# Thirty-seven low parts built by an accumulating transfer, and one modulation vector moved from TensorE to VectorE

## The chip, the cores and the metric

The program runs on one core of a Trainium2 chip. The metric is the device time of one execution in microseconds (us), here the median of three runs. Five engines work side by side, each through its own queue in order: TensorE (PE, with its weight loads as PEld), VectorE (DVE), ScalarE (ACT), GpSimd (POOL) and SyncE (SP), which here only issues transfers. Sixteen DMA engines move the data.

## The reference, cut to what is computed

Two groups of 128 tokens (context and latent) pass through two layers with the same weights. A layer is a half-step SwiGLU FFN, a token mixer of three branches (a Mamba-2 scan, differential attention, multi-scale pooling), and a second FFN. Each of the three sub-layers takes a normalised input that is shifted, scaled and gated by vectors made from the conditioning:

```
mod = silu(cond) @ w_ada[l] + b_ada[l]          # nine vectors of 1024
h = modulate(rmsnorm(x, g[0]), mod[0], mod[1])
x = x + 0.5 * mod[2] * swiglu(h, ffn_w_in[l, 0], ffn_w_out[l, 0])
h = modulate(rmsnorm(x, g[1]), mod[3], mod[4])
x = x + mod[5] * mixer(h)
h = modulate(rmsnorm(x, g[2]), mod[6], mod[7])
x = x + 0.5 * mod[8] * swiglu(h, ffn_w_in[l, 1], ffn_w_out[l, 1])
```

All weights are float32, and the whole of them is read once.

## The kernel before, in words

All weights of the products lie in HBM as 486 tiles of 128 x 1024 float32 (512 KB) in the order of their use (`plan`). The text numbers them 0 to 485. The order is, for each layer: 44 tiles `fin` (FFN input) and 22 `fout`, then the mixer's 111 tiles, then 44 `fin` and 22 `fout` again. The stretches that the change touches are the mixer of layer 0 from its keys on (tiles 113 to 168), the second FFN of layer 0 (177 to 242) and the first FFN of layer 1 (243 to 308).

A product is made with three matmuls in place of one. Each weight tile is split into a high part `wh` (a cast to float32r by ACT, `emit_hi`) and a low part `wl` (the raw tile minus the high part, by DVE, `emit_lo`), and the input into `xh` and `xl`; `mm3` adds wh·xh, wh·xl and wl·xh in PSUM. So a tile costs PE 24 matmuls, ACT one cast and DVE one subtraction.

SP loads the raw tiles into four buffers. High parts are made up to `HI_AHEAD` = 5 tiles and low parts up to `LO_AHEAD` = 4 tiles ahead of the tile that PE is to start next, both from `end`, which follows the issue of each tile's matmuls. `wh` and `wl` have five buffers each, so a cast for tile u waits until PE has done with tile u - 5. A raw buffer is free again when the subtraction has read it; the next load is asked for at that point (`load_more`).

The modulation vectors are made in two ways. `ada_stream` loads an eighth of one (512 KB, `wada`) and multiplies it on PE into the tile `pa` (four float32 matmuls, which the trace shows as eight rows). `ada_rows` loads an eighth of its transpose (`wrow`) and makes it on DVE: two `scalar_tensor_tensor` over 128 x 1024 with an accumulated sum, one for each group. The table `ROWS` lists the vectors (layer, number) made in this second way, and `CAP` how many of its eighths each stretch may take; whatever is left in the list goes to the next stretch.

Side work (modulation, norms, attention, the scan) is put between the tiles by `Pace`, a planner that keeps an estimated clock for each engine while the program is built. What it decides is fixed in the program: on the chip each queue runs in that order.

In a `fin` stretch the first pairs of tiles (`HYB` = 8 pairs, 16 tiles, in the stretches above) are multiplied before the row factors of the norm are known, and DVE puts these in when it reads PSUM (`wide`); beside them `full_h` makes the normalised input, eight pieces, each through POOL (`t1k<-x,rb`), DVE and ACT. The text calls these 16 tiles the hybrid stretch. The row factor itself passes through POOL (`rsr`, a power) just before it.

Of the kernel before, what the change touches and what calls it, by code (L numbers as in the profile page):

```python
# [12 lines left out]
AF = mybir.ActivationFunctionType  # L13
ALU = mybir.AluOpType
# [22 lines left out]
OFF_K = 3616  # L37
# [11 lines left out]
LO_AHEAD = 4  # L49
# [10 lines left out]
FIRST = 5.0  # L60
FH_ACT = False
FEED_ACT = 0
ROWS = ((0, 5), (0, 6), (0, 7), (0, 8), (1, 0), (1, 2), (1, 3), (1, 4), (1, 5), (1, 6), (1, 7), (1, 8))
CAP = {(0, 0): (5, 9), ("mix", 0): (18,), (0, 1): (16, 10), (1, 0): (16, 10), ("mix", 1): (18,), (1, 1): (12, 0)}
MIX_END = 2
MIX0 = 1
HOLD = 5
END = 6
ROW_LAG = 0.7
ROW_RAMP = 0.0  # L70
# [116 lines left out]
def ada_plan(seq):  # L187
# [5 lines left out]
    def spread(mods, u0, u1):  # L193
        items = [m + (k,) for m in mods if m not in ROWS for k in range(KD)]
        rest.extend((int(u0 + (u1 - u0) * j / len(items)), it) for j, it in enumerate(items))
# [13 lines left out]
def rows_plan(seq):  # L209
    def at(*head):  # L210
        return next(u for u, s in enumerate(seq) if s[:len(head)] == head)

    def even(n, a, b):
        return [a + j * (b - a) // n for j in range(n)]

    plan = {}
    for key, n in CAP.items():
        if key[0] == "mix":
            e = at("wout", key[1])
            us, last = even(n[0], at("win", key[1], OFF_K) + MIX0, e - MIX_END), e  # L220
        else:
            a = at("fin", *key)
            us = even(n[0], a + IN0, a + 2 * KF - 4) + even(n[1], a + 2 * KF, a + 3 * KF - END)
            last = a + 3 * KF
        plan[key] = us, last
    return plan


def pack_rows(w_ada):
    return np.stack([w_ada[l, :, i * D:(i + 1) * D].T.reshape(KD, P, D) for l, i in ROWS])  # L230

# [96 lines left out]
class Pace:  # L328

    LAT = {"pe": 0.25, "dve": 0.13, "act": 0.17, "pool": 0.2, "dma": 2.2}

    def __init__(self):
        self.clk = {"pe": 0.0, "dve": 0.0, "act": 0.0, "pool": 0.0, "dma": 0.0}
        self.wr = {}
        self.acc = {}
        self.last = {}
        self.born = {}
        self.slots = {}  # L340
# [22 lines left out]
    def op(self, eng, cost, outs, ins):  # L363
# [14 lines left out]
        for a in outs:  # L378
            r = self.wr.setdefault(a.tensor.name, {})
            lo, hi = self.span(a)  # L380
            for k in [k for k in r if lo <= k[0] and k[1] <= hi]:
                del r[k]
            r[lo, hi] = t + self.LAT[eng]

# [40 lines left out]
def backbone(ctx: ExitStack, tc: tile.TileContext, seq, wst, wada, wa0, wrow, xT_d, cT_d, cB_d, ck_d, cv_d, h0_d, prm_d, cst_d,  # L425
             y_d, nk_d, nv_d, ns_d):
    nc = tc.nc
    pace = Pace()
    clk = pace.clk
    V, S, T_, G = (Paced(pace, n, e) for n, e in  # L430
                   (("dve", nc.vector), ("act", nc.scalar), ("pe", nc.tensor), ("pool", nc.gpsimd)))
# [13 lines left out]
    def nm(s):  # L445
        uid[0] += 1
        return f"{s}{uid[0]}"
# [4 lines left out]
    def big(dt=F32):  # L452
        return bigx(dt)[:, 0:1024]
# [78 lines left out]
    def advance():  # L532
        again = True
        while again:
            again = False
            for lst, n in ((side["first"], 99), (side["gens"], CONC), (side["slow"], 99)):
                for s in list(lst[:n]):
                    if due(s) and step_side(s, lst):
                        again = True
                        break  # L540
                if again:
                    break
# [12 lines left out]
    def add(gen, first=False):  # L555
        side["first" if first else "gens"].append(Side(gen))

    def misc(gen):
        add(gen, True)

    raws = {}
    wt = {}
    st = {"load": 0, "cap": T0, "hi": 0, "lo": 0, "cur": 0}

    def load(out, src):
        nc.sync.dma_start(out=out, in_=src)
        pace.op("dma", out.free_size() * P * 4 / 360e3, [out], [])
# [5 lines left out]
    def load_more(limit):  # L573
        while st["load"] < min(limit, st["cap"]):
            i = st["load"]
            raws[i] = pace.slot("raw", RAW_BUFS, wp.tile([P, 1024], F32, tag="raw", bufs=RAW_BUFS, name=nm("raw")))
            load(raws[i], wst[i])
            st["load"] += 1

    def emit_hi():  # L580
        u = st["hi"]
        if u < T0:
            hi = big(F32R)
        else:
            hi = pace.slot("wh", WH_BUFS, wp.tile([P, 1024], F32R, tag="wh", bufs=WH_BUFS, name=nm("wh")))
        S.copy(hi, raws[u])
        wt[u] = [hi, None]
        st["hi"] += 1

    def emit_lo():  # L590
        u = st["lo"]
        if u < T0:
            lo = big(F32R)
        else:
            lo = pace.slot("wl", WL_BUFS, wp.tile([P, 1024], F32R, tag="wl", bufs=WL_BUFS, name=nm("wl")))
        V.tensor_tensor(out=lo, in0=raws.pop(u), in1=wt[u][0], op=ALU.subtract)
        wt[u][1] = lo
        st["lo"] += 1
        load_more(st["lo"] + RAW_BUFS)

    def use(desc):
        u = st["cur"]
        assert seq[u] == desc, (seq[u], desc)
        while st["hi"] <= u:
            emit_hi()
        while st["lo"] <= u:
            emit_lo()
        st["cur"] += 1
        hi, lo = wt.pop(u)
        return hi, lo  # L610

    def end(later=(), swap=False, less=0):
        cur = st["cur"]
        if not swap:
            for fn in later:
                fn()
            advance()
        while st["hi"] < min(cur + HI_AHEAD - less, len(seq)) and st["hi"] in raws:
            emit_hi()
        while st["lo"] < min(cur + LO_AHEAD - less, st["hi"]):  # L620
            emit_lo()
        if swap:
            for fn in later:
                fn()
        advance()
# [65 lines left out]
    row_plan = rows_plan(seq)  # L691
    row_todo = [m + (j,) for m in ROWS for j in range(KD)]

# [3 lines left out]
    def ada_rows(us, last):  # L697
# [10 lines left out]
        while True:  # L708
            if not row_todo or st["cur"] >= last - HOLD:
                us.clear()  # L710
            if us and len(loaded) < 2 and us[0] <= st["cur"] + 2:
                u, item = us.pop(0), row_todo.pop(0)
                raw = big()
                load(raw, wrow[ROWS.index(item[:2]), item[2]])
                loaded.append((u, item, raw))
# [164 lines left out]
    def ffn_in(l, f, box=None, pre=()):  # L880
# [47 lines left out]
        for p in range(KF):  # L928
            if p == HYB[l, f]:
                settle(lambda: "h" in box)  # L930
            if p % 2 == 0:
                cat.append(big(F32R))
            for which in range(2):
                ps = pre.pop(0) if pre else mtile(("fin", l, f, which * KF + p), hs if p >= HYB[l, f] else fh)
                pend.append((evac_u if which else evac_g, p, ps))
                later = []
                if box["rb"] is not None:
                    while pend:
                        fn, pi, t = pend.pop(0)
                        later += fn(pi, t)  # L940
                end(later, SWAP_I)
            if l == 0 and f == 0 and p == T_SIDE:
                side["slow"].append(Side(ada_rows(*row_plan[l, f]), row_lag))
                side["slow"].append(Side(ada_stream()))
            if l == 0 and f == 0 and p == T_SETUP:
                add(setup_consts())
                add(setup_layer(0))
        return out

    def ffn_out(l, f, acts, nxt):  # L950
# [3 lines left out]
        for m in range(KD):  # L954
            ps = pmain(2 * NT if m < KD - 1 else NT)
            for k in range(KF):
                if not cur:
                    if n:
                        end(later, SWAP_F, FO_LESS[max(0, n + 7 - KF)])
                        later = []  # L960
                    cur = tiles8(use(("fout", l, f, n)))
                    n += 1
                wh, wl = cur.pop(0)
                xh, xc = acts[k]
                if m == KD - 1:
                    T_.matmul(ps, lhsT=wh, rhs=xh, start=(k == 0), stop=False)
                    T_.matmul(ps, lhsT=wh, rhs=xc[:, NT:], start=False, stop=False)
                    T_.matmul(ps, lhsT=wl, rhs=xh, start=False, stop=(k == KF - 1))
                    if k % SUB == SUB - 1:
                        advance()  # L970
                    continue
                if k < KF - 1:
                    T_.matmul(ps, lhsT=wh, rhs=xc, start=(k == 0), stop=False)
                T_.matmul(ps[:, 0:NT], lhsT=wl, rhs=xh, start=False, stop=False)
                if k == KF - 1:
                    T_.matmul(ps, lhsT=wh, rhs=xc, start=False, stop=True)
                if k % SUB == SUB - 1:
                    advance()
            later += gated_add(l, 2 if f == 0 else 8, m, [ps[:, 0:NT], ps[:, NT:]] if m < KD - 1 else [ps], nxt, m == KD - 1)
        end(later)  # L980

    def setup_consts():
# [723 lines left out]
    def split():  # L1706
        emit_hi()
        emit_lo()
# [128 lines left out]
```

## Time and profile before

| | |
|---|---|
| median of three runs | 1553.76 us (1552.73 to 1557.59) |
| the profiled execution: its own time | 1555.05 us |
| its span, first to last instruction | 1553.2 us, TensorE's granted clock 0.998 of full |
| TensorE busy | 1513.9 us, 97% |
| VectorE busy | 1303.5 us, 84% |
| ScalarE busy | 864.5 us, 56% |
| GpSimd busy | 60.7 us, 4% |
| read from HBM | 342.00 MB, 223 GB/s over the span |

The span is what the trace covers, and 1.85 us of the execution's own time lie around it. Busy shares are means over the whole program; the stretches differ.

### The profile page before, as it was taken

What the parts mean: (1) busy time and instruction counts of PE and PEld (TensorE: products, weight loads), DVE (VectorE), ACT (ScalarE), POOL (GpSimd) and SP (SyncE); (2) the same over time, 40 slices, a digit from 0 to 9 for tenths busy, and PEclk for the clock granted to TensorE, in tenths of its full rate; (3) what the DMA queues carried; (4) which work ended last, traced back from release to release, by engine and by line L of the source; (5) the groups of instructions that cost most, each with busy time, mean ns of one, the idle gap of its engine ahead of it and who ended that gap; (6) DMA issues with size and microseconds to landing.
All of it is one profiled execution on the core that took longest, in us unless ns stands there. A gap on an engine that the chain in (4) does not pass through costs nothing. (4 is left out here: it accounts for less than half of the span.)

```text
span 1553.2 us, 30573 instructions
## 1 busy us (share of the span) xinstructions
PE 1513.9 (97%) x11934; PEld 1421.0 (91%) x11934; DVE 1303.5 (84%) x2404; ACT 864.5 (56%) x1560; POOL 60.7 (4%) x65
## 2 busy tenths in 40 slices
PE   6999999999999999999999999999999999999997
PEld 4998889989979999899899998998897999999986
DVE  5777798986888998899989999898778989998664
ACT  3564447665576446644446544577556744665442
POOL 0000002000001000100001000110000020010000
PEclk9999999999999999999999999999999999999999
DMA  9698775553765666688766887555467568568652
GB/s 373 224 338 287 264 265 166 188 187 131 246 214 190 220 240 221 209 297 286 265 215 200 288 279 269 189 179 186 158 213 229 189 204 287 172 201 279 211 181 82
DMA packets 103345, 350.30 MB, mean 226 GB/s; under 512 B 11424, under 2 KB 19232, under 8 KB 103072
## 3 DMA queue, kind: packets, MB, share of 16 engines
q1 hardware_dynamic: 103200, 348.34, 65.9%
q8 instruction: 94, 1.54, 0.4%
q14 instruction: 51, 0.42, 0.1%
HBM read 342.00 MB, written 4.19 MB: 223 GB/s over the span
## 5 line engine op out<-in xcount | busy, mean ns | idle before, releaser
L394 PE MATMUL pm<-big,wh 128*128 128x256 f32 (+2 forms) x6568 | 1289.6, 293 | 4.3 <-DVE big L394 2.5
L394 PEld LDWEIGHTS pm<-big,wh 128*128 128x128 f32 x6568 | 1028.0, 189 | 53.3 <-issue 20.2
L394 PE MATMUL pm<-big,wl 128*128 128x256 f32 (+1 forms) x3592 | 1003.6, 281 | 0.0
L394 PEld LDWEIGHTS pm<-big,wl 128*128 128x128 f32 x3592 | 676.6, 188 | 2.3
L394 DVE TENSOR_TENSOR wl<-raw,wh 128x1024 fp32r<-128x1024 f32 x481 | 587.8, 1227 | 14.8 <-ACT wh L394 14.4
L394 ACT CAST wh<-raw 128x1024 fp32r<-128x1024 f32 x481 | 502.5, 1050 | 137.4 <-PE pm L394 87.6
L394 DVE SCALAR_TENSOR_TENSOR big<-big,big 128x1024 f32<-128x1024 f32 x198 | 241.9, 1222 | 12.8 <-DMA big<-wrow 11.4
L394 ACT CAST big<-t1k 128x256 fp32r<-128x256 f32 x88 | 36.0, 409 | 156.3 <-DVE t1k L394 156.3
L394 PE MATMUL pm<-wh,big 128*128 128x512 f32 x256 | 86.2, 401 | 2.0 <-ACT big L394 2.0
L394 ACT ACTIVATE big<-x,amod 128x128 fp32r<-128x128 f32 x96 | 33.5, 397 | 96.7 <-DVE x L394 79.1
L394 DVE TENSOR_TENSOR wide<-pm,rb 128x258 f32<-128x258 f32 (+1 forms) x108 | 45.2, 422 | 36.8 <-PE pm L394 33.3
L394 DVE SCALAR_TENSOR_TENSOR x<-pm,mods,x 128x128 f32<-128x128 f32 x152 | 43.7, 345 | 36.4 <-PE pm L394 36.2
L394 PEld LDWEIGHTS pm<-wh,big 128*128 128x128 f32 x256 | 48.2, 188 | 15.0 <-ACT big L394 2.9
L394 ACT COPY big<-pm 128x256 f32<-128x256 f32 (+2 forms) x88 | 30.8, 374 | 50.3 <-PE pm L394 50.0
L394 DVE TENSOR_TENSOR big<-t1k,big 128x256 fp32r<-128x256 f32 x128 | 55.7, 440 | 1.6 <-ACT big L394 0.9
L394 ACT ACTIVATE t1k<-wide 128x128 f32<-128x128 f32 (+1 forms) x96 | 33.6, 397 | 38.9 <-DVE wide L394 38.6
L394 PE MATMUL pm<-wl,big 128*128 128x512 f32 x128 | 50.3, 393 | 0.0
L394 PE MATMUL s<-big,big 128*64 128x128 f32 (+5 forms) x416 | 46.3, 312 | 1.5 <-ACT big L394 1.5
L394 ACT ACTIVATE t1k<-pm 128x256 f32<-128x256 f32 x58 | 22.4, 386 | 43.8 <-PE pm L394 43.8
L394 POOL TENSOR_TENSOR rsr<-rsv,halfc 128x2 f32<-128x2 f32 x9 | 6.3, 698 | 919.0 <-DVE rsv L394 919.0
L394 DVE TENSOR_TENSOR t1k<-pm,t1k 128x256 f32<-128x256 f32 x42 | 17.8, 424 | 28.6 <-PE pm L394 26.7
L394 DVE SCALAR_TENSOR_TENSOR big<-big,cw,big 128x252 f32<-128x252 f32 (+1 forms) x96 | 39.4, 485 | 2.8 <-ACT big L394 2.8
(146 smaller groups left out, 977.7 us busy)
## 6 DMA issues: line engine op xcount, KB each, us to landing
raw<-wst SPq DMA_DIRECT2D x486, 512.0 KB, 4.2
big<-wrow SPq DMA_DIRECT2D x96, 512.0 KB, 5.6
big<-wada SPq DMA_DIRECT2D x32, 512.0 KB, 5.6
big<-wa SPq DMA_DIRECT2D x16, 512.0 KB, 10.2
big<-cB SPq DMA_DIRECT2D x12, 512.0 KB, 7.4
big<-big SPq DMA_DIRECT2D x32, 64.0 KB, 5.2
x<-xT SPq DMA_DIRECT2D x1, 1024.0 KB, 4.9
big<-h SPq DMA_DIRECT2D x2, 512.0 KB, 5.2
```

The source lines that it names most:

```text
L394: r = fn(*a, **k)
```

## The change

For 37 tiles (`DMA_LO`, `dma_plan`) DVE's subtraction is taken out. In its place ACT writes the negated high part into the `wl` buffer, and POOL issues a transfer that reads the raw tile from HBM a second time and adds it to what stands there. The raw buffer of such a tile is given back when the cast has read it. These tiles' low parts are begun one tile earlier than the others. They are 13 tiles in the mixer of layer 0 (115, 119, ... 163), 14 in the second FFN of layer 0 (181, 185, ... 233) and 10 in the first FFN of layer 1 (247, 253, ... 301). The vector (1, 1), eight eighths, joins `ROWS` and so goes from PE to DVE; `CAP` is the same. The planner gets a clock for the new transfers.

```diff
-ROWS = ((0, 5), (0, 6), (0, 7), (0, 8), (1, 0), (1, 2), (1, 3), (1, 4), (1, 5), (1, 6), (1, 7), (1, 8))
+ROWS = ((0, 5), (0, 6), (0, 7), (0, 8), (1, 0), (1, 1), (1, 2), (1, 3), (1, 4), (1, 5), (1, 6), (1, 7), (1, 8))
...
+DMA_LO = (
+    (("win", 0, OFF_K, 2), ("wout", 0, -4), 4),
+    (("fin", 0, 1, 4), ("fin", 0, 1, 60), 4),
+    (("fin", 1, 0, 4), ("fin", 1, 0, 60), 6),
+)
...
+def dma_plan(seq):
+
+    def at(*head):
+        return next(u for u, s in enumerate(seq) if s[:len(head)] == head)
+
+    plan = set()
+    for a, b, step in DMA_LO:
+        plan.update(range(at(*a[:-1]) + a[-1], at(*b[:-1]) + b[-1], step))
+    return plan
...
-    LAT = {"pe": 0.25, "dve": 0.13, "act": 0.17, "pool": 0.2, "dma": 2.2}
+    LAT = {"pe": 0.25, "dve": 0.13, "act": 0.17, "pool": 0.2, "dma": 2.2, "acc": 4.0}
...
-        V.tensor_tensor(out=lo, in0=raws.pop(u), in1=wt[u][0], op=ALU.subtract)
+        if u in by_dma:
+            raws.pop(u)
+            S.activation(out=lo, in_=wt[u][0], func=AF.Copy, scale=-1.0)
+            nc.gpsimd.dma_start(out=lo, in_=wst[u], accum_op=ALU.add)
+            pace.op("acc", 1.5, [lo], [lo])
+        else:
+            V.tensor_tensor(out=lo, in0=raws.pop(u), in1=wt[u][0], op=ALU.subtract)
...
-        while st["lo"] < min(cur + LO_AHEAD - less, st["hi"]):
+        while st["lo"] < min(cur + LO_AHEAD + (st["lo"] in by_dma) - less, st["hi"]):
```

The order of the instructions shows three places. The first is PE in the input stretch of layer 0's second FFN, tile 211, where the eighth and last item of vector (1, 1) stands before (`pa`).

```order
L394 MATMUL pm_8819<-big_7449,wh_8667 128x256
L394 MATMUL pm_8819<-big_7447,wl_8704 128x256
L394 MATMUL pa_7414<-big_8753,silc 32x256 x4
L394 MATMUL pm_8819<-big_7447,wh_8667 128x256
L394 MATMUL pm_8819<-big_7449,wh_8667 128x256
L394 MATMUL pm_8819<-big_7447,wl_8704 128x256
```

After the change no row with `pa` stands in this stretch; the eight before are at tiles 176 to 211.

The second is ACT in the hybrid stretch of layer 1's first FFN, at tile 253. Before:

```order
L394 CAST wh_10060<-raw_9905 128x1024
L394 ACTIVATE big_9827<-t1k_10042,mods_83,amod_85 128x128 x2
L394 CAST big_10013<-t1k_10055 128x256
L394 CAST wh_10104<-raw_9956 128x1024
L394 ACTIVATE t1k_10136<-wide_10137 128x128 x2
L394 CAST wh_10141<-raw_10002 128x1024
```

And of the change:

```order
L410 CAST wh_10053<-raw_9898 128x1024
L410 ACTIVATE big_9824<-t1k_10029,mods_83,amod_85 128x128 x2
L410 CAST big_10006<-t1k_10048 128x256
L410 CAST wh_10097<-raw_9949 128x1024
L410 ACTIVATE wl_10103<-wh_10097 128x1024
L410 ACTIVATE t1k_10137<-wide_10138 128x128 x2
L410 CAST wh_10142<-raw_9995 128x1024
```

The negation stands right behind its cast, ahead of the SiLU of the next pair.

The third is POOL at the start of layer 0's second FFN: the row factor (`rsr`), the pieces of `full_h` (`t1k<-x,rb`) and, of the change, the transfers of tiles 181 and 185.

```order
L616 DMA wl_7499<-wst 128x1024
L410 TENSOR_TENSOR rsr_7509<-rsv_7507,halfc 128x2
L410 TENSOR_TENSOR t1k_7601<-x,rb_7564 128x256
L410 TENSOR_TENSOR t1k_7603<-x,rb_7564 128x256
L616 DMA wl_7646<-wst 128x1024
L410 TENSOR_TENSOR t1k_7653<-x,rb_7564 128x256
```

Before, POOL's queue has no transfer at all; now the row factor stands behind one, and the third to eighth piece of `full_h` behind another.

## Rows read from the trace of the kernel before

**Rows 1.** Page, parts 1 and 2: busy us (share) xinstructions; GB/s in 40 slices.
```profile
PE 1513.9 (97%) x11934; PEld 1421.0 (91%) x11934; DVE 1303.5 (84%) x2404; ACT 864.5 (56%) x1560; POOL 60.7 (4%) x65
PEclk9999999999999999999999999999999999999999
GB/s 373 224 338 287 264 265 166 188 187 131 246 214 190 220 240 221 209 297 286 265 215 200 288 279 269 189 179 186 158 213 229 189 204 287 172 201 279 211 181 82
```

**Rows 2.** Waits of PE: us in total, times, longest us.
```profile
PE pa L394 <- DMA big<-wada: 4.6, 5, 1.3
...
PE pm L394 <- DVE wide L394: 1.7, 6, 0.5
```

**Rows 3.** PE's instructions on tile pa, 596 to 725 us.
```profile
L394 PE MATMUL pa<-big,silc x64: 379/391/403, 603.5 to 715.9; 128*32 128x256 f32 x64
```

**Rows 4.** Timeline of PE at 715 us: start us, us, instruction.
```profile
715.47 0.28 PE L394 MATMUL pm<-big,wl 128*128 128x256 f32 x1
715.68 0.64 PE L394 MATMUL pa<-big,silc 128*32 128x256 f32 x8
716.25 0.50 PE L394 MATMUL pm<-big,wh 128*128 128x256 f32 x2
716.59 0.28 PE L394 MATMUL pm<-big,wl 128*128 128x256 f32 x1
```

**Rows 5.** Groups of instructions, shapes apart: busy us, mean ns | idle before.
```profile
L394 DVE TENSOR_TENSOR wl<-raw,wh 128x1024 fp32r<-128x1024 f32 x481 | 587.8, 1227 | 14.8 <-ACT wh L394 14.4
L394 DVE SCALAR_TENSOR_TENSOR big<-big,big 128x1024 f32<-128x1024 f32 x198 | 241.9, 1222 | 12.8 <-DMA big<-wrow 11.4 <-ACT big L394 0.4
...
L394 ACT ACTIVATE big<-big 128x1024 f32<-128x1024 f32 x18 | 18.7, 1058 | 0.4 <-DVE big L394 0.4
...
L394 DVE DVE_READ_ACCUMULATOR big<-big,big 128x1 f32 x192 | 16.2, 85 | 0.0
```

**Rows 6.** Windows: stretch, PE, PEld, DVE, ACT, POOL busy us, PEclk, DMA share, GB/s.
```profile
615.00:650.00 35.00, 33.14 (x272) 31.12 (x271) 32.00 (x66) 24.98 (x49) 5.97 (x8) 1.00 0.64 211
655.00:742.70 87.70, 85.46 (x735) 82.52 (x734) 77.30 (x122) 39.36 (x60) 0.00 (x0) 1.00 0.83 293
815.00:850.00 35.00, 34.78 (x291) 34.61 (x291) 33.84 (x69) 24.34 (x47) 4.78 (x7) 1.00 0.58 192
```

**Rows 7.** Transfers of the raw tiles: KB each, median us to landing; their range.
```profile
raw<-wst SPq DMA_DIRECT2D x486, 512.0 KB, 4.2
DMA to landing us min/median/max: 3.4/4.2/11.2
```

**Rows 8.** Timeline of ACT: the casts of tiles 189, 209 and 253.
```profile
638.88 1.05 ACT L394 CAST wh<-raw 128x1024 fp32r<-128x1024 f32 x1
...
696.37 1.05 ACT L394 CAST wh<-raw 128x1024 fp32r<-128x1024 f32 x1
...
829.45 1.06 ACT L394 CAST wh<-raw 128x1024 fp32r<-128x1024 f32 x1
```

**Rows 9.** Timeline of PE: first matmul with wl of tiles 189, 209 and 253.
```profile
645.88 0.29 PE L394 MATMUL pm<-big,wl 128*128 128x258 f32 x1
...
708.08 0.28 PE L394 MATMUL pm<-big,wl 128*128 128x256 f32 x1
...
834.63 0.28 PE L394 MATMUL pm<-big,wl 128*128 128x258 f32 x1
```

**Rows 10.** Timeline of POOL and DVE at 825 us, layer 1's hybrid stretch.
```profile
825.18 0.74 POOL L394 TENSOR_TENSOR t1k<-x,rb 128x256 f32<-128x256 f32 x1 [1.30 <-DVE t1k L394]
...
825.25 1.75 DVE L394 TENSOR_TENSOR wl<-raw,wh 128x1024 fp32r<-128x1024 f32 x1
...
829.02 1.22 DVE L394 TENSOR_TENSOR wl<-raw,wh 128x1024 fp32r<-128x1024 f32 x1
```

More of the change, by code (lines that the diff above doesn't have):

```diff
@@ L328 @@
 class Pace:
-    LAT = {"pe": 0.25, "dve": 0.13, "act": 0.17, "pool": 0.2, "dma": 2.2}
+    LAT = {"pe": 0.25, "dve": 0.13, "act": 0.17, "pool": 0.2, "dma": 2.2, "acc": 4.0}
     def __init__(self):
-        self.clk = {"pe": 0.0, "dve": 0.0, "act": 0.0, "pool": 0.0, "dma": 0.0}
+        self.clk = {"pe": 0.0, "dve": 0.0, "act": 0.0, "pool": 0.0, "dma": 0.0, "acc": 0.0}
         self.wr = {}
@@ L559, in misc @@
         add(gen, True)
+    by_dma = dma_plan(seq)
     raws = {}
```

## The prediction, made before the run

> **What bounds the kernel now.** I read the page's busy line and slices first. TensorE is busy 97% of the span, 1513.9 of 1553.2 us, at a clock of 9 tenths or more in every slice [rows 1]; VectorE has 84% and ScalarE 56%. So the end is set by TensorE's work plus the few microseconds in which it waits, and anything else counts only where it makes TensorE wait. The waits of PE come next. One entry is tied to what the change touches: the items of vector (1, 1) wait for their loads, 4.6 us in five waits, the longest 1.3; waits on VectorE's `wide` are 1.7 us in six [rows 2]. No wait for a `wl` or a `wh` is large enough to stand there. The windows show where a second engine is close: VectorE is busy 32.0 of 35 us and 33.84 of 35 in the two hybrid stretches, and 77.3 of 87.7 in the rest of layer 0's second FFN; ScalarE has at least 10 us free in each [rows 6].
>
> **What PE loses: 10.1 us.** The eight items are the 64 rows of `pa` from 603.5 to 715.9 us [rows 3]. Row busy times overlap on PE, so I take starts. From the matmul ahead of the last item (715.47) to the one behind it (716.25) pass 0.78 us [rows 4]; without it two neighbours start some 0.12 apart (1513.9 us of PE over 11934 matmuls are 0.127 each [rows 1]). So an item costs 0.66, eight 5.3. With them go the waits for their loads, 4.6 [rows 2], and two small transposes of the finished vector, some 0.2 together. Sum 10.1. These loads become eight of the same size in the same queue, `wrow` for `wada`, so I price the bytes at nothing.
>
> **What VectorE, ScalarE and SP get: nothing, under cover.** VectorE loses 37 subtractions of 1.227 and gains 16 row products of 1.222 with a read of 0.085 behind each [rows 5]: -45.4 + 20.9 = -24.5 us. It is covered already outside the hybrid stretches, and no row product of the eight falls inside one. ScalarE gains 37 negations. The nearest row is its 128 x 1024 activation, 1.058 us [rows 5], so +39; the negation reads float32r in place of float32, and I see no reason for less. In the busiest place it goes from 24.98 to about 30 of 35 us. If that cover is gone, each negation makes the evacuation behind it 1.06 late. The raw buffer is given back by the cast, about 2 us earlier than by the subtraction, which can only help the next load.
>
> **POOL.** Its queue had no transfer among these pieces; now the row factor stands behind tile 181's and six pieces of `full_h` behind 185's. Each transfer must wait for its negation, and what stands behind it waits too. Both negations come well before the pieces are needed; I price it at 0, and at up to 2 us for the range.
>
> **The new wait: 4.1 us.** A low part was made 1.2 us after its cast; now it takes a negation and a transfer of which no row exists. Call L the time from the end of the negation to the landing. Bounds are the shortest and the longest landing of a raw tile of the same 512 KB, 3.4 and 11.2 [rows 7]. I start at their median, 4.2. To add, the transfer must also read what stands in `wl`: 0.52 MB at the highest rate of any slice, 373 GB/s [rows 1], is 1.4; a handover between the engines 0.2. L = 5.8, near the lower bound because the median is.
>
> What a tile can afford is the first matmul with its `wl` less the end of its cast less 1.06. For tile 209, a steady one: 708.08 - (696.37 + 1.05) - 1.06 = 9.6 [rows 8, 9]. In the same way from the casts and first matmuls of all 37, 33 lie between 8.2 (tile 229) and 13.0 (tile 143). Four, in the hybrid stretches, are short. Tile 253: 834.63 - 830.51 - 1.06 = 3.06. Tile 189: 645.88 - 639.93 - 1.06 = 4.89; two items ahead of it are gone, 1.7 plus waits of 0.5, so PE is there 2.2 us earlier, while its cast comes 1.7 earlier (one subtraction of 1.75, beside POOL, is gone): about 4.4. Tile 259 has 4.95, and gains 1.65 by 253's subtraction and by the wait at 253. Tile 185 has 6.66, less 0.8 for PE's earlier arrival. At L = 5.8 tile 253 waits 2.7 and tile 189 1.4; 185 and 259 just hold. That is 4.1.
>
> The same list gives the price at other L (a wait lengthens the budget of the next such tile by as much): 1.2 at 4.2, 5.0 at 6.1, 6.8 at 7, 8.8 at 8, then 17 at 9 (15 tiles late), 25 at 9.5 (22 late) and 52 at 11. It is nearly flat until the steady tiles begin to be late, between 8.2 and 9, and steep after.
>
> **The term on `wide`: -0.9.** Of PE's 1.7 us [rows 2] about half lies in the stretches that VectorE gets relief in; I take 0.9.
>
> **Sum.** -10.1 + 4.1 - 0.9 = -6.9. The profiled execution took 1555.05: 1553.2 of span and 1.85 around it, 1.29 above the median of the runs. So 1548.2 for a profiled execution of the same sort, and 1546.9 to the median: I say 1547.0.
>
> **A rule of the pages against it.** Beside a POOL piece that started at 825.18, a subtraction took 1.75 us; a later one alone 1.22 [rows 10]. So POOL and VectorE hinder each other here, by 0.5 us. The Trainium skill ("SBUF — State Buffer", "SBUF: two separate sides") says that GpSimd writes the descriptors of the transfers it issues through ports that it shares with VectorE, and that a VectorE operation in a two-port mode locks it out; its example goes from about 620 to about 3100 ns. The trace agrees that the two engines collide, and does not show a transfer held up. What it would do is the third rival below. The same notes ("DMA: Bandwidth & Descriptors", "Anatomy of one DMA — SWDGE (gpsimd) path") fit such a transfer as 2.0 us plus the bytes at 436 GB/s; an estimate from that page for 512 KB is 3.2, and by it tile 253 alone would wait, some 0.1, and the sum would be -10.9, 1543. My L is the higher one because raw tiles take 4.2 here [rows 7].
>
> **The rivals.** *Quick transfers:* L below 5. Then B is 1.2 to 2.5, time 1543 to 1545.5. For: 3.4 is the shortest landing. Against: the median, and the second operand. Chance 0.12.
>
> *What is freed is handed back:* the two items in layer 0's hybrid stretch (at about 622 and 642 us) make up some 2.9 of the 10.1. VectorE works 32 of 35 there [rows 6] and PE cannot outrun it; PE then waits on `wide` for those 2.9, and the time is 1550 to 1551. Against: three or four subtractions, 4 to 5 us, leave VectorE in just this stretch. Chance 0.08.
>
> *Each transfer is issued late.* If an issue on POOL is held by one or two VectorE operations of 1.22, L is 7.0 to 8.3, B 6.8 to 10, the time 1550 to 1553. Or the transfers' second reads fill the DMA engines: from 655 to 742 their share is 0.83 at 293 GB/s [rows 6]. All engines busy would be 293 / 0.83 = 353 there, if the highest slice did not show 373 [rows 1]. Seven transfers of two reads in 87.7 us add 84 GB/s and make 377, or 362 if I take off the loads of `wada` whose successors lie elsewhere: 2.5 to 7% over, 2 to 6 us, 1549 to 1553. Chance of both 0.20.
>
> *Slower.* L past 8.9: the steady tiles come late, 15 at once, and B passes 15.6, which takes the gain and 0.3% more. At 9.5 it is 25, which gives 1567 to 1568. For: 11.2 has been seen for a raw tile [rows 7], and a queue of POOL with pieces, issues and VectorE's collisions in it is slower than SP's. Against: steady tiles have no POOL work beside them, and one longest landing in 486 is not a median. Chance 0.15.
>
> **How the numbers follow.** The forecast, L from 5 to 7 with the rest as above, is 1543.5 to 1550, chance 0.45, and the predicted time is its 1547. Quick 0.12, handed back 0.08, late or full 0.20, slower 0.15. A measurement of this kernel can tell about 0.3% from no change: faster is below 1549.1, slower above 1558.4. Faster: quick and nearly all of the forecast, 0.54. Slower: 0.15 and a little of late, 0.16. The same 0.30. The range from 1541.5 (L at its lower bound, where only tile 253 waits, 0.3: 1543.1, and the rest of the `wide` waits and the measurement's own spread off) to 1560 leaves the rest of the slow cases out.
>
> **What would show it.** In the profile after: no `pa` rows from 596 to 725 us and the loads' 4.6 us gone from PE's waits; VectorE's busy time near 1279, ScalarE's near 904; a transfer row of POOL, 37 of 512 KB, with a median landing of 5 to 7; a PE wait on the transfer of `wl` of about 4 us in two or three waits, the longest at tile 253. A median landing over 8.2 with such waits at steady tiles makes the prediction wrong on the slow side; no wait on `wl` at all, on the fast. `wide` growing over 3 us means handed back; raw tiles landing much later than 4.2 in 655 to 742 means full engines.

## The result, and the profile after

The changed kernel takes 1601.68 us (median; 1596.43 to 1608.45), the kernel before beside it 1553.24: a ratio of 1.0299, 95% interval 1.0273 to 1.0325. It is 48 us slower. The profiled execution took 1608.45 us, 53.4 more than the one of before (1555.05).

The page, parts 1, 3 and 6: busy us (share) and instructions; queues with packets, MB and share of 16 engines' span; issues with KB and median us to landing.

```profile
PE 1532.3 (95%) x11868; PEld 1440.6 (90%) x11868; DVE 1284.1 (80%) x2397; ACT 899.7 (56%) x1597; POOL 93.1 (6%) x102
...
q1 hardware_dynamic: 103200, 348.34, 63.6%
q0 software_dynamic: 5328, 19.40, 6.5%
...
raw<-wst SPq DMA_DIRECT2D x486, 512.0 KB, 4.4
big<-wrow SPq DMA_DIRECT2D x104, 512.0 KB, 6.7
wl<-wst POOLq DMA_DIRECT2D x37, 512.0 KB, 9.0
```

TensorE has 66 matmul instructions fewer than before [rows 1] and is busy 18.4 us longer. VectorE is down by 19.4 us and ScalarE up by 35.2, near the 24.5 and 39 of the forecast. The new transfers (queue q0, POOL's) land 9.0 us after their issue. A packet of theirs takes 6.5% of 1606.5 x 16 us over 5328, that is 314 ns; one of the loads (q1) takes 158.

PE's waits: us in total, times, longest us.

```profile
PE pm L410 <- DMA wl<-wst: 32.2, 14, 4.6
PE s L410 <- DVE sqa L410: 10.5, 1, 10.5
PE s L410 <- ACT big L410: 6.8, 2, 6.0
...
PE pm L410 <- DVE wide L410: 1.4, 1, 1.4
```

The waits for `wada` (4.6 us) are gone [rows 2], and 32.2 us of waits for low parts have come, far more than the 4.1 of the forecast. The 10.5 us on `sqa` lie in the program's start and stand in every run (10.4 to 10.9). The 6.0 us on ScalarE are in layer 0's mixer.

Windows (columns as in [rows 6]) of the two hybrid stretches and, in the middle, the steady tiles of layer 0's second FFN:

```profile
625.00:660.00 35.00, 29.10 (x227) 28.68 (x226) 26.15 (x60) 24.16 (x46) 7.74 (x10) 0.95 0.70 193
665.00:756.00 91.00, 84.41 (x670) 83.80 (x669) 70.11 (x115) 44.74 (x66) 5.14 (x6) 0.95 0.91 288
845.00:882.00 37.00, 34.63 (x274) 34.42 (x273) 29.64 (x64) 26.04 (x48) 6.32 (x8) 0.95 0.71 224
```

VectorE did get room in the hybrid stretches (26 of 35 us in place of 32; as PE gets through fewer matmuls in such a window now, count the same tiles, 177 to 193: 38.3 us in place of 44.6). The granted clock is 0.95 in place of 1.00, and the DMA engines' share in the steady tiles is 0.91 in place of 0.83 [rows 6].

One late tile, 213, in the timeline (SP, ACT, POOL and PE; start us, us, instruction, [wait]):

```profile
729.42 1.06 SPq L583 DMA_DIRECT2D raw<-wst  x2
730.54 0.89 SPq L583 DMA_DIRECT2D big<-wrow  x2
...
728.61 1.05 ACT L410 CAST wh<-raw 128x1024 fp32r<-128x1024 f32 x1
729.69 1.06 ACT L410 ACTIVATE wl<-wh 128x1024 fp32r<-128x1024 f32 x1
...
731.05 0.86 POOL L616 DMA_DIRECT2D wl<-wst  x1 [13.51 <-ACT t1k L410]
...
738.98 0.40 PE L410 MATMUL pm<-big,wh 128*128 128x256 f32 x2
742.09 0.39 PE L410 MATMUL pm<-big,wl 128*128 128x256 f32 x1 [2.72 <-DMA wl<-wst]
...
743.10 0.42 PE L410 MATMUL pm<-big,wl 128*128 128x256 f32 x1
743.32 0.63 PE L410 MATMUL pm<-big,wh 128*128 128x256 f32 x2
743.74 0.41 PE L410 MATMUL pm<-big,wl 128*128 128x256 f32 x1
```

Read it from the top. The cast ends at 729.66 and gives its raw buffer back, and between 729.4 and 731.4 SP asks for two raw tiles and two eighths of rows, four times 512 KB. POOL's issue at 731.05 comes right behind the last of them. It lands 11.0 us later. PE wants the low part 2.7 us before that. Behind the wait three matmuls take 0.64 us (743.10 to 743.74), where three take 0.36 at full clock.

Windows around a long and around a short wait show when that happens (same columns):

```profile
658.00:662.20 4.20, 0.00 (x0) 0.00 (x0) 4.10 (x8) 3.27 (x7) 0.00 (x0) 0.82 1.00 256
662.20:667.50 5.30, 5.22 (x24) 5.22 (x25) 0.09 (x2) 1.01 (x1) 0.86 (x1) 0.50 0.90 306
...
946.00:947.10 1.10, 0.03 (x1) 0.00 (x0) 1.10 (x2) 0.74 (x2) 0.00 (x0) 1.00 0.98 387
947.10:950.00 2.90, 2.82 (x23) 2.82 (x24) 2.90 (x6) 0.61 (x1) 0.00 (x0) 1.00 1.04 424
```

After a wait of 4.6 us the granted clock is 0.50, the lower of its two levels (1.2 GHz): 24 matmul rows in 5.3 us. After a wait of 1.2 us it stays at 1.00. Past the first 60 us of this run the nine waits of 2.4 us or more (eight on low parts and the one of 6.0) were followed by half clock, and none of the six others on low parts, 1.2 or less; before, no such stretch lies ahead of the program's last 10 us. By the trace's clock records PE worked 38 us at half clock (the program's end, which is the same in both, left out), so an estimated 19 us went there. In other versions the line isn't that sharp: e4 below has waits of 2.6 and 2.7 us with 1.00 behind them, and e6 two of 1.8 us with half clock behind them. The second of e4's:

```profile
985.00:987.30 2.30, 0.00 (x0) 0.00 (x0) 1.74 (x4) 1.27 (x2) 0.00 (x0) 1.00 1.01 369
987.30:991.00 3.70, 3.68 (x21) 3.25 (x22) 1.94 (x3) 1.05 (x1) 0.00 (x0) 1.00 1.04 423
```

Where the 53.4 us are:

| | us |
|---|---|
| PE waits for low parts | +32.2 |
| matmuls at half clock | +19.0 |
| PE's `s` waiting for ScalarE, 6.8 in place of 1.5 (the 6.0 us wait in the mixer) | +5.3 |
| the eight items with their waits, as forecast | -10.1 |
| left, not traced to a cause | +7.0 |

### The profile page after: what moved, and what is told of

It reads as the page before. It is cut to its first block, busy times and chain, and to the rows that moved or that the text cites. A ratio compares the mean times of both kernels' runs of the same rounds, so it can differ in the third digit from the quotient of the medians.

```text
span 1606.5 us, 30527 instructions
## 1 busy us (share of the span) xinstructions
PE 1532.3 (95%) x11868; PEld 1440.6 (90%) x11868; DVE 1284.1 (80%) x2397; ACT 899.7 (56%) x1597; POOL 93.1 (6%) x102
## 3 DMA queue, kind: packets, MB, share of 16 engines
q0 software_dynamic: 5328, 19.40, 6.5%
## 4 chain that ended last, share of the span: by engine, by line
PE 63%; issue 19%; DMA 10%; DVE 5%; ACT 2%; POOL 1%; SPq 0%; DVEq 0%; POOLq 0%; ACTq 0%
PE pm L410 56%; DMA wl<-wst 6%; PE s L410 5%; DMA big<-wrow 2%; DVE big L410 2%; PE pa L410 1%; DVE wl L410 1%; DVE t1k L410 1%; DMA big<-big 1%; ACT big L410 1%; ACT wh L410 1%; DMA nk<-big 1%; POOL wl L616 0%; POOL osr L410 0%; DMA x<-xT 0%
## 5 line engine op out<-in xcount | busy, mean ns | idle before, releaser
L410 PE MATMUL pm<-big,wh 128*128 128x256 f32 (+2 forms) x6568 | 1305.2, 296 | 3.9 <-DVE big L410 2.5
L410 PEld LDWEIGHTS pm<-big,wh 128*128 128x128 f32 x6568 | 1040.7, 190 | 48.1 <-issue 15.5
L410 PE MATMUL pm<-big,wl 128*128 128x256 f32 (+1 forms) x3592 | 1014.0, 284 | 32.2 <-DMA wl<-wst 32.2
L410 PEld LDWEIGHTS pm<-big,wl 128*128 128x128 f32 x3592 | 684.1, 190 | 38.2 <-DMA wl<-wst 35.7
L410 DVE TENSOR_TENSOR wl<-raw,wh 128x1024 fp32r<-128x1024 f32 x444 | 540.9, 1223 | 13.6 <-ACT wh L410 12.9
L410 DVE SCALAR_TENSOR_TENSOR big<-big,big 128x1024 f32<-128x1024 f32 x214 | 261.2, 1220 | 45.0 <-DMA big<-wrow 42.6
L616 POOL DMA_DIRECT2D wl<-wst x37 | 32.4, 875 | 640.4 <-ACT wl L410 265.1
L410 PEld LDWEIGHTS s<-big,big 128*128 128x128 f32 (+2 forms) x416 | 36.1, 178 | 12.3 <-ACT big L410 8.0
## 6 DMA issues: line engine op xcount, KB each, us to landing
big<-wa SPq DMA_DIRECT2D x16, 512.0 KB, 10.1
```

The costliest lines, as they stand in the source:

```text
L410: r = fn(*a, **k)
L616: nc.gpsimd.dma_start(out=lo, in_=wst[u], accum_op=ALU.add)
```

## Experiments

The first theory, **queue and budget**: the transfers stand among other transfers on the DMA engines, land later than PE's budget (the time from the end of a tile's negation until PE wants the part), and each long wait brings half clock behind it. Its rivals: **starvation** (VectorE holds up what POOL has to do for a transfer), **rows** (the 16 more row products are the trouble), and later **load** (the traffic is, whoever waits for it). The diffs are against the changed kernel unless said.

| label | us | ratio to before (95%) | wl waits, us (times) | landing, us |
|---|---|---|---|---|
| the change | 1601.7 | 1.0299 (1.0273 to 1.0325) | 32.2 (14) | 9.0 |
| e1_rows_only | 1602.8 | 1.0303 (1.0276 to 1.033) | 30.0 (3), on DVE | none |
| e2_lo_only | 1603.9 | 1.0309 (1.0275 to 1.0343) | 25.2 (16) | 9.1 |
| e3_plain | 1570.4 | 1.0087 (1.0054 to 1.0119) | 12.6 (8) | 7.0 |
| e4_raw_held | 1593.1 | 1.0251 (1.0211 to 1.029) | 24.4 (14) | 6.9 |
| e6_neg_first | 1601.3 | 1.0292 (1.0262 to 1.0322) | 30.4 (15) | 8.4 |
| e7_half | 1601.2 | 1.0305 (1.0256 to 1.0354) | 23.8 (10) | 9.2 |
| e10_no_mixer | 1602.4 | 1.0301 (1.0262 to 1.034) | 27.2 (16) | 8.8 |
| e8_pool_sub | 1609.9 | 1.0348 (1.0316 to 1.0379) | 16.6 (3), on DVE | none |
| f1_wl_last | 1589.3 | 1.0214 (1.017 to 1.0257) | 18.5 (15) | 9.2 |
| f2_wl_last_neg_first | 1598.0 | 1.0282 (1.0258 to 1.0305) | 26.1 (13) | 8.3 |
| f3_before_wl_last | 1561.6 | 1.0034 (1.002 to 1.0048) | none | none |
| g1_plain_wl_last | 1558.3 | 1.0013 (1.0001 to 1.0025) | 4.2 (5) | 7.2 |
| g2_idle_traffic | 1567.3 | 1.0066 (1.0041 to 1.0091) | none | 7.0 |

### e1_rows_only and e2_lo_only: the two halves of the change

```diff
 e1:
-DMA_LO = ((("win", 0, OFF_K, 2), ...
+DMA_LO = ()
 e2:
-ROWS = (..., (1, 0), (1, 1), (1, 2), ...
+ROWS = (..., (1, 0), (1, 2), ...
```

> Vector (1, 1) on VectorE, all low parts by VectorE's subtraction. Three theories of the 48 us. Queue: the accumulating transfers stand behind other transfers on the DMA engines, and their packets take twice as long (328 against 159 ns); without them this kernel is 8 to 10 us under the kernel before, 1543 to 1546. Starvation: VectorE holds up POOL's issue of them; the same 1543 to 1546 here. Rows: the 16 more row products, their loads and the order that the planner makes for them cost time; then this kernel is slower than before, 1560 or more.

> The 37 accumulating transfers, with vector (1, 1) left on TensorE. Queue: some 10 us more than the whole change, 1603 to 1613, or a few less since fewer loads of rows lie in the two stretches; landings still near 9 us. Starvation: less VectorE work, so landings nearer 8.5 and 1595 to 1610. Rows: about the time before, 1550 to 1560.

Either half alone costs what both cost together. The losses stand in different places, so that the sums agree is chance as far as these runs show. e1's time is what the rows theory expected, and far from the 1543 to 1546 of the two others. In e1 TensorE does get its gain first: it starts tile 176 1.3 us behind the kernel before, and tile 212 at 707.7 us, where before it was 717.1, so 9.4 ahead: 10.6 gained over the eight items. Then VectorE falls due. PE's waits and VectorE's queue in e1:

```profile
PE pm L406 <- DVE wl L406: 30.0, 3, 15.4
PE pm L406 <- DVE x L406: 12.7, 1, 12.7
```
```profile
760.29 1.22 DVE L406 SCALAR_TENSOR_TENSOR big<-big,big 128x1024 f32<-128x1024 f32 x1
761.44 0.08 DVE L406 DVE_READ_ACCUMULATOR big<-big,big 128x1 f32 x1
761.56 1.22 DVE L406 SCALAR_TENSOR_TENSOR big<-big,big 128x1024 f32<-128x1024 f32 x1
...
764.61 1.21 DVE L406 TENSOR_TENSOR wl<-raw,wh 128x1024 fp32r<-128x1024 f32 x1
```

The planner finds no room for all row products inside the stretches and puts what is left at their ends: 13 of them in one piece ahead of a subtraction at tile 227, 13 at tile 293 and 8 at 415 (counted in the order of the program). PE waits for the subtraction behind the first two (15.4 and 14.3 us) and for `x` behind the third (12.7). Not all of this is VectorE's work: inside the pieces VectorE waits for loads of rows itself, 4.9, 4.2 and 6.5 us. The last of these:

```profile
1374.01 1.23 DVE L406 SCALAR_TENSOR_TENSOR big<-big,big 128x1024 f32<-128x1024 f32 x1 [6.50 <-DMA big<-wrow]
```

In the changed kernel no such piece is left, the longest is of four products: the removed subtractions make the room. So the rows theory holds for e1 and not for the change. In e2 the time lies in the ranges of queue and of starvation; the transfers land as late as in the change (9.1 us), which is nearer to queue's 9 than to starvation's 8.5, and the loads that the vector's items wait for come late too (`PE pa` on `wada` 11.1 us in place of 4.6), which is why the items on TensorE cost more there than they did before.

### e3_plain and e4_raw_held: what a transfer takes, and what stands ahead of it

```diff
 e3:
-            nc.gpsimd.dma_start(out=lo, in_=wst[u], accum_op=ALU.add)
+            nc.gpsimd.dma_start(out=lo, in_=wst[u])
 e4:
-            raws.pop(u)
+            raw = raws.pop(u)
             ...
             nc.gpsimd.dma_start(out=lo, in_=wst[u], accum_op=ALU.add)
+            nc.gpsimd.tensor_copy(out=hold[:, 0:1], in_=raw[:, 0:1])
```

> The transfers copy the raw tile and don't add to what stands in the buffer, so the low parts are not low parts; count, bytes from HBM, queue and order are the same. Queue: 4 KB packets near 159 ns, the landing after the issue falls from 9.0 to 6.5 to 7.2, PE's waits on the transfers from 32 to 5 to 12 us, time 1550 to 1562. Starvation: what lies ahead of the first packet stays at 3.9 us, the landing falls by no more than the 1.3 us that the packets take less, to 7.7, and the time is 1555 to 1570.

> As the change, but POOL copies one element of the raw tile behind the issue of each accumulating transfer, so the raw buffer is given back only then and its next load comes behind the transfer in place of 1.2 us ahead of it. Queue: the first packet 2.0 to 2.8 us after the issue in place of 3.9, landing 7.0 to 7.8 in place of 9.0, PE's waits on it 5 to 15 us, time 1553 to 1572. Starvation: the order of the loads changes nothing, landing 9 and time 1595 to 1605; more if the copy holds POOL.

e3, part 3 of the page and PE's waits:

```profile
q0 software_dynamic: 5328, 19.40, 3.6%
```
```profile
PE pm L410 <- DMA wl<-wst: 12.6, 8, 4.4
```

3.6% of 1569.4 x 16 us over 5328 packets is 170 ns, near a load's 158. So adding doubles the time that a packet takes on the DMA engines, and 31 of the 48 us go when it is left out. The first packet comes 2.6 us after the issue (median), where starvation expected 3.9 as in the change, and the landing of 7.0 is in queue's range and under starvation's 7.7. The time of 1570 decides nothing: it is over queue's 1562 and at the upper end of starvation's range. A landing of 7.0 us is still too long for the tight tiles (the wait of 4.4 is tile 189's).

e4, one transfer and its copy on POOL, and the landings, of e4 and, last, of the change:

```profile
710.39 0.86 POOL L617 DMA_DIRECT2D wl<-wst  x1 [12.59 <-ACT t1k L410]
710.93 0.59 POOL L618 COPY hold<-raw 128x1 f32<-128x1 f32 x1
```
```profile
DMA to landing us min/median/max: 5.2/6.9/9.6
...
DMA to landing us min/median/max: 5.4/9.0/11.0
```

The packet records say why it lands 2.1 us earlier: the median of the time from issue to first packet is 1.6 us (24 of 37 under 1.7) where it was 4.0 in the change (2 under 1.7). VectorE's work is the same in both, so starvation falls: it was the raw loads, asked for ahead of the transfer, that it stood behind. But the time went down by 8.6 us only, to 1593 against the 1553 to 1572 expected, and the waits to 24.4 against 5 to 15: the raw tiles now come later (ScalarE's casts wait 36.9 us for them in place of 22.9), and the budgets shrink with them (median 8.2 us in place of 9.2). The queue is the same engines' work in another order.

### e6_neg_first, e7_half, e10_no_mixer and e8_pool_sub: earlier, fewer, elsewhere, without

```diff
 e6: in emit_hi, for the 37 tiles
+            S.activation(out=lo, in_=raws[u], func=AF.Copy, scale=-1.0)
+            nc.gpsimd.dma_start(out=lo, in_=wst[u], accum_op=ALU.add)
         S.copy(hi, raws[u])
 e7: steps 8, 8 and 12 in DMA_LO in place of 4, 4 and 6
 e10:
-    (("win", 0, OFF_K, 2), ("wout", 0, -4), 4),
 e8:
-            S.activation(...); nc.gpsimd.dma_start(...)
+            G.tensor_tensor(out=lo, in0=raws.pop(u), in1=wt[u][0], op=ALU.subtract)
```

> As the change, but ACT makes the negation from the raw tile ahead of the cast in place of behind it, so the transfer is issued 1.05 us earlier and the raw buffer, which the cast gives back, is reloaded behind the issue in place of ahead of it. Queue and late budgets: first packet 1.6 to 2.5 us after the issue, landing 7.0 to 7.8, budgets 1.05 longer; PE's waits on the transfers 5 to 14 us in place of 32, time 1555 to 1575. If the loss were in the number of transfers alone, however they are ordered, 1590 to 1605.

> Every second of the transfers (19 in place of 37), vector (1, 1) still on VectorE. Late transfers each at its own tile: landing still 8 to 9 us, waits on them 13 to 18 us, half as many stretches at half clock, time 1565 to 1580. If the loss comes from DMA engines that are full over the stretch, it falls by more than half: 1550 to 1562. If VectorE lacks room for the row products, new waits on VectorE come up and the time stays over 1585.

> The 24 transfers of the two FFN stretches alone, none in the mixer. The trace of the change puts 10.3 us of its loss into the mixer (one wait of 6.0 on ScalarE behind a late raw tile, 1.5 on a transfer, 3 at half clock). If these come from the transfers there: 1588 to 1594. If from the products of rows that lie in the mixer: 1598 to 1604.

> The 37 low parts made by a subtraction on POOL, with no second read of the raw tile and no negation. POOL's piece of 256 columns took 0.74 us, so about 3 us for 1024, and VectorE's operations beside it 1.75 in place of 1.22. If lateness of the transfers is what costs, no wait on a low part is left in the steady tiles, and the time is 1545 to 1565, where the upper end is from 6 and 8 row products that stand in one piece in VectorE's order. If POOL and VectorE hold each other up for all of it, VectorE gains nothing, and 1570 or more.

All four missed the time that the first theory expected, and each met that of a rival: e6 that of the number of transfers alone (1590 to 1605), e7 that of a VectorE without room for the row products (over 1585), e10 that of the row products in the mixer (1598 to 1604), e8 that of POOL and VectorE holding each other up (1570 or more). In e6 the first packet does come 1.9 us after the issue (median), but the transfer then shares the engines with the raw loads asked for beside it, and its packets take 5.8 us from first to last (median) in place of 4.5. Landing moved by 0.6 us in all. Order among the transfers moves the wait about; it doesn't remove it.

e7 and e10 show the other half again. PE's waits in e7 and in e10:

```profile
PE pm L410 <- DMA wl<-wst: 23.8, 10, 6.9
...
PE pm L410 <- DVE x L410: 7.0, 1, 7.0
```
```profile
PE pm L409 <- DMA wl<-wst: 27.2, 16, 4.9
...
PE pm L409 <- DVE x L409: 7.8, 1, 7.8
```

With half of the transfers each one is as late as before (9.2 us), so it is not their number that makes them late, and the subtractions that VectorE has again leave four row products to the end of layer 1's mixer, where PE waits 7.0 us on `x`; VectorE itself waits 6.0 us there for a load of rows (6.7 in e10). e1, e6, e7 and e10 come out within 2 us of the change with different shares of late transfers and late row products, and no run shows why the sums agree. e10 does answer its own question: without transfers in the mixer PE starts tile 177 0.7 us behind the kernel before, against 10.4 in the change, so that part of the loss came from the transfers there; the row products bring it back elsewhere.

In e8 a subtraction on POOL took 2985 ns (median), but VectorE's row products rose to a mean of 1335 ns over the program from 1222 [rows 5], and PE waited 16.6 us on VectorE's subtractions and 13.0 on `x`. POOL and VectorE do hold each other up, and it is the slowest version of all. But the waits of 10.0 and 13.0 stand behind six and eight row products in one piece, at tiles 293 and 415 as in e1, so how much of the loss is the holding up is not shown.

### f1_wl_last, f2_wl_last_neg_first and f3_before_wl_last: the time at which the low part is wanted

```diff
-        for k, (wh, wl) in enumerate(tiles):   # wh.xh, wh.xl, wl.xh for each piece
+        todo = [(k, j) for k in range(n) for j in (0, 1)] + [(k, 2) for k in range(n)]   # n == 8
+        for i, (k, j) in enumerate(todo):
+            T_.matmul(ps, lhsT=tiles[k][j == 2], rhs=hs[k][j == 1], ...)
```

> As the change, but in each product of a tile with eight pieces the eight matmuls with the low part come behind the sixteen with the high part, in place of one in each piece; so the low part is wanted 1.9 us later (16 matmuls of 0.12) and nothing else is changed. Late transfers with a short budget: landing still about 9, waits on the transfers 32 - 14 x 1.9, some 6 to 13 us, at most three stretches at half clock, time 1556 to 1576. If the loss is in the load on the DMA engines whatever the budget: 1590 to 1605.

> The low part's matmuls last, and the negation ahead of the cast: 3 us more of budget than in the change. Late transfers: waits 3 to 8 us, one or two stretches at half clock, time 1548 to 1566; that is below the kernel before only if the mixer's 5 us and the hybrid stretches' waits go too. Load on the DMA engines: 1590 to 1605.

> The kernel before, with the low part's matmuls last, as the control for the two others. No wait for a low part is there to be saved, so 1551 to 1557; if the order of the matmuls by itself slows TensorE or moves the side work, more, and the two others are read against it.

f1 takes 12 us off with landings at 9.2 as before: the waits fall to 18.5 us, and PE at half clock loses 8.2 us in place of 19.0. That is what budgets predict in kind, but its 1589 misses the 1556 to 1576 expected and lies at the edge of what the load theory expected (1590 to 1605): the median budget is longer by 0.9 us (10.0 in place of 9.2), not by 1.9. That an earlier PE asks for the next tiles earlier too would explain this; it is not shown. The control f3 is 0.34% slower than the kernel before, some 5 us that f1 may carry as well. f2 should have been better than f1 and is not, and its 1598 is inside the load theory's range. Its transfers take 5.7 us from first to last packet, as in e6, and ScalarE waits 46.3 us for raw tiles, 21.1 in f1; whether that is the 9 us is left open. So these three don't decide between waits and load.

### g1_plain_wl_last and g2_idle_traffic: both remedies, and the traffic alone

```diff
 g1: e3 and f1 together
 g2, against the kernel before:
+            nc.gpsimd.tensor_copy(out=sink[:, 0:1], in_=wt[u][0][:, 0:1])
+            nc.gpsimd.dma_start(out=sink, in_=wst[u][:, 0:704], accum_op=ALU.add)
         V.tensor_tensor(out=lo, in0=raws.pop(u), in1=wt[u][0], op=ALU.subtract)
```

> The plain copies (no addition, so the low parts are not low parts) together with the low part's matmuls last. If lateness against a budget is what counts, both remedies add up: landing 7, waits on it 1 to 4 us in place of 12.6, no half clock in the steady tiles, time 1550 to 1562 against 1570 and 1589 for either alone (the matmul order itself costs 5). If each only uncovers another wait: 1568 or more.

> The kernel before (all subtractions on VectorE, twelve vectors), and behind the cast of each of the 37 tiles POOL issues an accumulating transfer of 704 of the raw tile's 1024 columns into a buffer that nobody reads. The traffic of the change without anyone waiting for it. If the cost is TensorE's wait for late low parts and the half clock behind it: 1553 to 1562. If the load on the DMA engines makes the raw tiles and rows late by itself: 1575 or more. For the mixer alone, 10 us of the change's loss: it stays if it is late raw tiles, and is gone if it is ScalarE's negations.

PE's waits in g1 and in g2:

```profile
PE pm L410 <- DMA wl<-wst: 4.2, 5, 1.1
```
```profile
PE pa L410 <- DMA big<-wada: 9.2, 6, 2.8
```

g1 is as expected: a landing of 7.2 us against a budget 1.9 us longer leaves waits of at most 1.1 us, no steady tile is followed by half clock, and the time is that of the kernel before to 0.13%. So with the time to land and the time at which the part is wanted nearly all of the loss goes. Not quite all: 10.1 us of work are gone too, and with 5 for the order of the matmuls and 4.2 of waits the time should be 2 to 3 us lower still. g2 came out above its expectation for the wait theory (1567 against 1553 to 1562) and well under that for the load: 0.66%, some 10 us, with 69% of the bytes. Its loss is in places that the change doesn't have, the waits for `wada` (9.2 us in place of 4.6) and the half clock behind three of them (an estimated 5). In the mixer it lost 1.3 us at most (casts from tile 108 to 156) where the change lost 10.8, so this traffic alone is not the mixer's loss. Nor are the negations alone: e3 has them all and lost 3.8 there. As e3 and g1 lighten the DMA engines too, what speaks against the load by itself is g2 and the account of the waits in the change's own trace.

## Why the prediction was wrong

**The removed work was right.** -10.1 forecast; e1 shows -10.6 over the stretch of the eight items, where nothing else has yet come in. VectorE's 1279 and ScalarE's 904 us came out as 1284.1 and 899.7, and no wait that could be a price for ScalarE's share in the FFN stretches or for POOL's order stands among PE's.

**The step that failed is "L = 5.8, near the lower bound because the median is".** The packets alone would have allowed it: 128 of them at 328 ns on 16 engines are 2.6 us, and my terms held as much (128 at a load's 159 ns, in the 4.2, are 1.3, and the second read was 1.4). What I left out is what stands ahead. The time from issue to first packet is 4.0 us (1.6 in most transfers of e4, where the raw loads come behind), and the packets are spread over 4.5 us by other transfers among them. With 0.3 for the handover, taken as 0.2 from no row, and 0.5 behind the last packet it came to 9.3 us from the end of the negation (median; 5.7 to 11.3), and 23 of 37 lie past the 8.9 that I had named as the point from which it decides. That was the last rival, at 0.15; it had 1567 to 1568 for an L of 9.5, so it too is far under what was measured. The median landing of raw tiles was the wrong neighbour: these are asked for when a buffer comes free, singly, while the transfer is asked for at the moment at which the change itself releases loads.

**"about 2 us earlier than by the subtraction, which can only help the next load" was wrong, and it is the same mistake.** It put the raw loads in front of the transfer (tile 213's rows above).

**The price of a wait was too low.** My list gave 17 us at L = 9 and 25 at 9.5 (done over by its own rule, from the casts and first matmuls of before: 15 and 20.5, and 18.5 at the 9.3 that came). The waits were 32.2. The list has one L for all tiles; with each tile's own it gives 23.8. And at six of the eight long waits the budget was 0.7 to 2.7 us shorter than before. The longest wait was not at tile 253 but at 189, where the budget was 3.7; behind the wait of 2.4 at tile 247, tile 253 had 8.0 and didn't wait. Half clock added 19, which no term held. Between its first 60 and its last 10 us the profile of before has no wait over 1.3 us, so its clock of 1.00 there said nothing of what a longer one would cost.

**The rivals.** Full engines I had at 2 to 6 us: right as the mechanism (the share rose from 0.83 to 0.91, and to 1.00 while PE waits for a transfer, and raw tiles landed there in 5.3 us in place of 4.4), wrong in that I priced it by throughput and not by the lateness that it gives each transfer. Starvation is not what happened: in e4 24 of 37 transfers start 1.6 us after their issue under a busy VectorE. The Trainium skill has that trap for VectorE operations in a two-port mode ("SBUF — State Buffer", "SBUF: two separate sides"); of `tensor_tensor`, VectorE's subtraction here, it says that it has no such mode and wasn't seen to stall transfers ("Who interferes with whom"), and e4's trace agrees. The Trainium skill's fit for such a transfer ("DMA: Bandwidth & Descriptors", "Anatomy of one DMA — SWDGE (gpsimd) path") gives 3.2 us for 512 KB as an estimate; the shortest landings of any run are longer, 3.9 without the addition (g1) and 5.2 with it (e4), and the measured ones decide. What was handed back in the hybrid stretch I had as `wide` over 3 us (the two items there are worth 2.5 by their rows, not my 2.9). It is nothing: the one wait of 1.4 us on `wide` stands at 1417 us, in layer 1's second FFN, and the 1.2 us of before in the two stretches are gone, where I had taken 0.9.

**Open** stay the 7.0 us that are left, how the mixer's 6.0 us wait divides between negations and late raw tiles, and f2. No version beat the kernel before.

## What to carry to other kernels

A transfer that PE waits for is priced from what is on the engines at the moment of its issue, not from the median landing of other transfers: look at what the same release sets off. Compare its time to land with the shortest time from issue to use at the steady tiles, and when many tiles have the same budget, treat a miss there as one for all of them. A part of a change can be there to make room for another: take it apart before judging either, since here each half alone lost as much as the whole, at other places.

## What the runs showed of the hardware

An accumulating transfer into SBUF takes the DMA engines twice as long per packet: 328 against 159 ns (medians for 4 KB; 174 for a plain copy from the same queue). Its issue holds POOL for 862 ns, against 530 for the plain copy. TensorE's granted clock fell to half behind each wait of 2.4 us or more in the changed kernel past its first 60 us, so a wait of 2.7 us at tile 213 cost an estimated 4.4 (with 3.4 us of work at half clock behind it). Over all versions no length of a wait divides the cases: waits of 2.6 and 2.7 us in e4 and one of 3.0 in f1 were followed by full clock, two of 1.8 in e6 by half.
